# A hybrid decoder layer on one core: the probabilities' transposes split over the two row halves of the array

## The chip, the core and the metric

One program on one core of a Trainium2 chip. TensorE multiplies (a stationary operand is loaded by LDWEIGHTS, a moving one is streamed through) and writes only to PSUM, here eight banks of 128 partitions x 512 float32. VectorE (DVE), ScalarE (ACT) and GpSimd (POOL) do the elementwise work, SyncE (SP) issues the transfers. The metric is the device time of one execution in microseconds, as the median of the runs shown. A profile is the record of one more execution.

## The reference, cut to what matters

One layer of a decoder: a combined input projection, two mixers (gated DeltaNet, and dilated sliding-window attention in three patterns), one output projection, a gated MLP with a short convolution, a final norm. Sequence 1024, width 1024, everything in float32. The change touches the second mixer only: 8 heads of 64, whose three branches are merged by their softmax denominators.

```python
DIL_PATTERNS = ((128, 1), (512, 4), (2048, 16))
BAND_BLOCK = 128

def band_attention(q, k, v, n_back):
    ...
    s = jnp.einsum('...nqd,...nkd->...nqk', qb, kk)
    ...
    s = jnp.where(valid, s, -jnp.inf)
    m = jnp.max(s, axis=-1)
    p = jnp.exp(s - m[..., None])
    den = jnp.sum(p, axis=-1)
    num = jnp.einsum('...nqk,...nkd->...nqd', p, vv)

def dilated_attention(q, k, v):
    ...
    out = num_tot / den_tot[..., None]
```

## The kernel before, in words

**Who sets the order.** The kernel is written as Python generators ("streams": input projection `dense`, delta-rule `chain`, `attention`, `out_proj`, MLP and others), which a small planner, `Weave` (lines 46 to 118), runs against a clock of its own. Each product on TensorE moves that clock by a cost given by hand (`wv.product`); each call on another engine is booked with a cost and a lag until its result is seen (`wv.account`). A stream that yields a number is looked at again when the clock has moved by that much; of all streams that are due, the one with the lowest level goes first. Attention has level 5, `out_proj` 8, `dense` 9. The order in which products are written is TensorE's order on the chip; it is fixed before anything runs. The other engines' order is made by the framework's scheduler from the data dependences, a priority (the wrappers `uv` and `ua` put attention's instructions ahead) and a few orderings written by hand (`after`).

Bookkeeping is by whole tiles: `need(tile)` is the time until the last booked write of a tile can be seen, and a further write to the same tile is booked behind it. VectorE's cost is 0.07 + 0.00105 us per element of a partition, ScalarE's 0.12 + 0.00085, the lag of both 0.28; a product's result is booked as seen 0.25 after it.

**Dense work.** `dense` goes through 25 column tiles of the input projection. Each has two halves of eight steps, and a step is three products of 128 x 128 by 128 x 512 (float32 split into a high and a low part, `mm3`: high x high, high x low, low x high). After each step the stream yields 0.0, so three products are the smallest piece that other streams can come between. They show in the profile as `ps<-xhi,whi`, `ps<-xlo,whi`, `ps<-xhi,wlo`. Four columns of the gate z come last; when a z column is through, `gate` multiplies it into a head's output (`zz`, `og`).

**Attention.** Four head pairs (`pi`), each with eight blocks of 128 queries (`n`), in two groups of four (`hh`), in pairs of blocks (`u` = 0 and 2). A block sees `wd` = 128 to 512 keys: one or two local blocks (`n1`) and `nb` = 0, 1 or 2 blocks of more distant keys, by `CBLOCKS`. The four pairs of blocks of a head pair are thus 128 and 256, 384 and 384, 384 and 384, 512 and 512 keys wide. `advance` pipelines them:

- `turn` (line 969) transposes the probabilities of the pair before, `sm` [queries, keys], to [keys, queries]. For each block (tags `asc` and `atr`) and each of its two heads (`e`) it takes a bank, transposes `wd`/128 squares into it (`tp`, one instruction each, `ps<-ident,sm`: the square is the stationary operand, the identity is streamed), and `turned` copies the local part with VectorE to `pt` and the distant part with ScalarE to `pb`. Ahead of every bank it yields until the block's softmax is due, less 1.0 for the first block and 0.6 for the second (`TSLACK`), so dense steps may come in between.
- `att_values`, once per head pair, transposes the next head pair's values.
- `scores` (line 909) takes four banks, two of each tag, waits until all are free, and multiplies queries by keys, the two heads of the pair on the two row halves of the array (64 rows each), into two banks. Then comes the `softmax` of each block: four fused mask-and-minimum passes on VectorE, four exponentials on ScalarE, four scalings on VectorE.
- `values` (line 983) multiplies the turned probabilities with the values, the two heads on two column halves; after the last pair of a group `merge_classes` adds the distant parts from `pb` (`ps<-pb,vc`), and `give` writes the group out (`oT`).

Each of the tags `asc`, `atr`, `hf`, `ch` has two banks. The four banks of a turn and the four of the next scores are the same four.

**After it.** `mixer_splits` starts when `dense` has written all its products. It splits each head's output into a high and a low part (`ohi`, `olo`), one head after another; inputs 0 to 3 come from the gated heads, 4 to 7 from attention. `out_proj` may start when the last group of attention has begun (`"last group"`): first with the first of its output tiles (j = 0), and with the second (j = 1) only when attention is done. A block of it is one input by one output tile, two halves of three products. In `turned`, for the very last block, three kinds of hand-written orderings hold VectorE's later work behind the last copy: the low parts of the first output weights (`wlo`), the multiplication of the last gate (`og`), and the low parts of all but the first split head (`olo`).

Of the kernel before, what the change touches and what calls it, by code (L numbers as in the profile page):

```python
# [144 lines left out]
def hybrid_layer(tc, I, out):  # L145
# [46 lines left out]
    def tp(dst, src):  # L192
        tc.stamp_issue_order_token(nc.tensor.transpose(dst, src, ident).ins, TOKEN)  # L193
        wv.product(0.11, dst, src)

# [49 lines left out]
    def bank(tag, name="ps"):  # L245
        return tile_(pp_, (P, 512), F32, name, tag, 2)
# [643 lines left out]
    def attention():  # L890
# [64 lines left out]
        def turned(it, e, pt, pp):  # L955
            wd, n1_ = it["wd"], it["n1"]
            inst = uv.tensor_copy(pt[:, :n1_], pp[:, :n1_])
            if it["g"]["pi"] == 3 and it["n"] == 7 and e == 1:

                lows = last.get("wlo", [])  # L960
                last["probabilities"] = inst
                for lo in lows:
                    after(lo, inst, "the probabilities go first")
                for slow in last["og"] + last.get("olo", [])[1:]:
                    after(slow, (lows or [inst])[0], "the first weights go first")
            if it["nb"]:
                ua.activation(it["pb"][e][:, it["u"], :it["nb"]].rearrange("p b t -> p (b t)"), pp[:, n1_:wd], AF.Copy)

        def turn(pair):
            pts = A("pt", "dv*", shape=(P, 4, 256))  # L970
            for b, (it, tag) in enumerate(zip(pair, ("asc", "atr"))):
                sm, wd, n1_ = it["sm"], it["wd"], it["n1"]
                it["pt"] = []
                for e in range(2):
                    pt = pts[:, 2 * b + e, :]
                    it["pt"].append(pt)
                    pp = bank(tag)
                    yield wv.need(pp, sm, slack=TSLACK[b])
                    for i in range(wd // P):
                        tp(pp[:, i * P:(i + 1) * P], sm[:, e, i * P:(i + 1) * P])  # L980
                    turned(it, e, pt, pp)
# [10 lines left out]
        def merge_classes(g):  # L992
# [3 lines left out]
            for c in range(4):  # L996
                for b in range(nb):

                    us = slice(2 if b == nb - 1 else 0, 4)
                    for e in range(2):  # L1000
                        er = slice(64 * e, 64 * e + 64)
                        mm(po[er].rearrange("p (u t) -> p u t", u=4)[:, us, 32 * c:32 * c + 32],
                           vcv[:, c, b, er], g["pb"][e][:, us, b, 32 * c:32 * c + 32], 0.14 if us.start == 0 else 0.08,
# [32 lines left out]
        for pi in range(4):  # L1036
            q, k, vn, vc = cur
            for hh in range(2):
# [5 lines left out]
                pb = [A("pb", "qa", shape=(P, 4, nb, P)) for _ in range(2)]  # L1044
# [50 lines left out]
    def out_proj():  # L1095
# [7 lines left out]
        while todo:  # L1103
# [7 lines left out]
            m, w = MORDER[j], ws[j]  # L1111
            if k == H and not third:
# [610 lines left out]
```

## Time and profile before

| | us |
|---|---|
| median of 3 runs | 1219.16 |
| lowest, highest | 1219.05, 1222.35 |
| the profiled execution | 1219.62 |
| its span | 1217.6 |
| granted TensorE clock over the span | 0.997 |
| attention's head pairs 1 to 4, from the first scores of one to those of the next | 41.9, 41.4, 41.4, 43.1 |
| TensorE busy with transposes in these stretches (line 193, values' transposes included) | 7.36, 7.41, 7.41, 6.37 |

How the rows are read. On the page, "PE" is TensorE's matmuls, "PEld" its weight loads; a busy time is followed by its share of the span and the number of instructions. A timeline row is: start, length, engine, line, operation, output <- inputs by the program's names, shape of the array used (rows*columns) and of the moving operand, and how many instructions the row merges; in brackets stands idle time ahead of it and what ended it. A matmul's length contains its way through the array, so matmuls overlap, and their pace is read from starts. A row of a group is: line, engine, operation, names and shape, count, then busy time, mean length in ns, and idle time before. A row of a stretch is: from:to, length, then for each engine the busy time and (count), the clock, the share of the DMA engines, GB/s. A tile's row is: count, shortest/median/longest ns, first and last start. The chain of waits has start, length, engine and work. Products all stand on line 189 or 193, elementwise work on 139 and 141, because helpers record them.

### The profile page before, as it was taken

The page shows a single profiled execution, that of the slowest core. Times are in us where ns is not written, and L with a number is a line of the kernel's source. Part 1 is how long each engine was busy: PE and PEld are TensorE (multiplying, and loading weights), DVE is VectorE, ACT ScalarE, POOL GpSimd, SP SyncE. Part 2 cuts the span into 40 slices and gives each one's busy share as a digit, 9 for nine tenths or more (in the row PEclk, how much of TensorE's full clock was granted, in tenths as well). Part 3 has the DMA queues.
Part 4 walks back from the last instruction along what each step waited for, and adds up shares of the span by engine and source line. Part 5 has one row for each costly group of instructions (what it writes and reads, how often), then busy time and mean ns, then how long its engine had stood idle before and what let it go on. Part 6 is the DMA issues. An engine that isn't in the chain of part 4 may idle for free.

```text
span 1217.6 us, 17960 instructions
## 1 busy us (share of the span) xinstructions
PE 1202.1 (99%) x6878; PEld 995.2 (82%) x6878; DVE 962.3 (79%) x1531; ACT 576.2 (47%) x1112; POOL 48.0 (4%) x34
## 2 busy tenths in 40 slices
PE   9999999999999999999999999999999999999996
PEld 7888887898777787888788888888888888888886
DVE  7686984474666678667888989888898889898987
ACT  7383344363444344555544445444454454445451
POOL 0212110022000000000000000000000000000000
PEclk9999999999999999999999999999999999999998
DMA  7323235336432312434123131231322296357734
GB/s 234 105 74 101 86 111 167 106 104 216 157 120 90 112 55 97 173 129 151 53 91 99 58 104 60 97 97 59 104 60 97 89 372 222 114 181 224 236 99 142
DMA packets 81846, 153.51 MB, mean 126 GB/s; under 512 B 21568, under 2 KB 32480, under 8 KB 81760
## 3 DMA queue, kind: packets, MB, share of 16 engines
q1 hardware_dynamic: 81760, 152.37, 38.2%
q8 instruction: 54, 0.88, 0.3%
q14 instruction: 32, 0.26, 0.1%
HBM read 114.31 MB, written 35.93 MB: 123 GB/s over the span
## 4 chain that ended last, share of the span: by engine, by line
PE 90%; DVE 4%; DMA 2%; issue 1%; ACT 1%; POOL 0%; SPq 0%; POOLq 0%; DVEq 0%; ACTq 0%
PE ps L189 44%; PE pa L189 19%; PE dw L189 14%; PE pc L189 10%; PE ps L193 3%; DVE x1h L139 1%; DVE pr L139 1%; DMA wst<-in_w 1%; DMA wst<-in_wu 1%; DVE rstdB L139 0%; DVE sm L141 0%; DMA xt<-in_xT 0%; DMA wst<-in_wo 0%; POOL rs L139 0%; DMA wba<-in_wba 0%
## 5 line engine op out<-in xcount | busy, mean ns | idle before, releaser
L189 PE MATMUL dw<-pr 128*128 128x512 f32 (+1 forms) x984 | 211.4, 376 | 0.0
L189 PEld LDWEIGHTS dw<-pr 128*128 128x128 f32 x984 | 176.7, 188 | 33.6
L189 PE MATMUL ps<-xhi,whi 128*128 128x512 f32 x448 | 186.8, 417 | 0.0
L189 PE MATMUL ps<-xhi,wlo 128*128 128x512 f32 x448 | 175.8, 392 | 0.4 <-DVE wlo L139 0.4
L189 PE MATMUL ps<-xlo,whi 128*128 128x512 f32 x448 | 174.8, 390 | 0.0
L189 PE MATMUL pa<-T,pair 128*128 128x512 f32 x528 | 127.1, 389 | 0.0
L189 PEld LDWEIGHTS pa<-T,pair 128*128 128x128 f32 x528 | 99.0, 188 | 20.4
L189 PEld LDWEIGHTS ps<-xhi,wlo 128*128 128x128 f32 x448 | 84.1, 188 | 19.3 <-DVE wlo L139 0.8
L189 PEld LDWEIGHTS ps<-xhi,whi 128*128 128x128 f32 x448 | 84.3, 188 | 16.7 <-issue 2.7
L189 PEld LDWEIGHTS ps<-xlo,whi 128*128 128x128 f32 x448 | 84.6, 189 | 13.2
L139 ACT ACTIVATE u<-pa 128x512 f32<-128x512 f32 x44 | 26.3, 599 | 109.8 <-PE pa L189 109.8
L139 DVE SCALAR_TENSOR_TENSOR y<-xu,fcw,y 128x1023 f32<-128x1023 f32 (+1 forms) x44 | 56.4, 1281 | 25.7 <-ACT y L139 25.6
L139 ACT ACTIVATE pr<-wd 128x1024 fp32r<-128x1024 f32 x33 | 35.0, 1061 | 77.0 <-DVE wd L139 37.5
L139 ACT ACTIVATE whi<-wst 128x1024 fp32r<-128x1024 f32 (+2 forms) x38 | 38.5, 1013 | 67.1 <-PE ps L189 58.9
L189 PE MATMUL pc<-T,S 128*128 128x512 f32 x264 | 63.4, 389 | 0.0
L189 PE MATMUL pa<-T,S 128*128 128x512 f32 x264 | 63.4, 389 | 0.0
L189 PE MATMUL pc<-B,pair 128*128 128x512 f32 x264 | 63.4, 389 | 0.0
L189 PE MATMUL pa<-B,A 128*128 128x512 f32 x264 | 63.4, 389 | 0.0
L139 DVE TENSOR_TENSOR wst<-wst 128x512 f32<-128x512 f32 x88 | 60.4, 686 | 0.8
L189 PE MATMUL ps<-B,pair 128*128 128x512 f32 x252 | 60.5, 389 | 0.0
L141 ACT ACTIVATE sm<-sm,mx 128x384 f32<-128x384 f32 (+3 forms) x64 | 37.8, 592 | 45.5 <-DVE mx L141 45.5
L189 PEld LDWEIGHTS pa<-T,S 128*128 128x128 f32 x264 | 49.6, 188 | 10.3
(235 smaller groups left out, 2275.8 us busy)
## 6 DMA issues: line engine op xcount, KB each, us to landing
wst<-in_wu SPq DMA_DIRECT2D x44, 512.0 KB, 3.7
wd<-in_wd SPq DMA_DIRECT2D x44, 512.0 KB, 4.4
wst<-in_wi SPq DMA_DIRECT2D x25, 512.0 KB, 3.7
upark<-y SPq DMA_DIRECT2D x22, 512.0 KB, 3.7
r<-upark SPq DMA_DIRECT2D x22, 512.0 KB, 9.4
apark<-aqkv SPq DMA_DIRECT2D x12, 512.0 KB, 2.8
wa<-in_wd SPq DMA_DIRECT2D x22, 256.0 KB, 2.9
wst<-in_wo SPq DMA_DIRECT2D x8, 512.0 KB, 3.8
```

Source lines behind the costliest of these rows:

```text
L139: return getattr(eng, op)(*a, **kw)
L141: return getattr(eng, op)(*a, **kw)
L189: tc.stamp_issue_order_token(nc.tensor.matmul(dst, lhs, rhs, start=start, stop=stop, **kw).ins, TOKEN)
L193: tc.stamp_issue_order_token(nc.tensor.transpose(dst, src, ident).ins, TOKEN)
```

## The change

A transpose of 128 queries becomes two of 64, one for the upper and one for the lower 64 rows of `sm` (`HALVES`), each with its own square of the identity (64 x 64). The halves of one block go to its two banks, a bank now holding 64 queries of both heads instead of 128 queries of one. Transposes of the two halves are written alternately, first all of block one, then all of block two, without a yield in between. Ahead of them all stands one wait: until both blocks' softmax is due and the four banks are free, less 0.6. The planner's cost of a half is 0.035. A VectorE copy takes both heads' 64 queries of the local keys; a ScalarE copy takes both heads' 64 queries of one distant key block, so a block with two of them has four such copies instead of two. The tiles `pb` are made per distant block, [keys, 4 blocks, 2 heads, queries], instead of per head. The three orderings behind the last copy are left out when a product of the output projection has already been written.

```diff
--- before.py
+++ after.py
@@ -192,6 +192,11 @@
     def tp(dst, src):
         tc.stamp_issue_order_token(nc.tensor.transpose(dst, src, ident).ins, TOKEN)
         wv.product(0.11, dst, src)
+
+    def tp_half(dst, src, rows):
+
+        tc.stamp_issue_order_token(nc.tensor.transpose(dst, src[rows], ident[rows, rows]).ins, TOKEN)
+        wv.product(0.035, dst, src)
 
     def mm3(dst, lhs, rhs, first, last, **kw):
         us = 0.2135 * rhs[0].shape[-1] / 512
@@ -952,33 +957,43 @@
                 div = uv.tensor_scalar(sm[:, e, :wd], sm[:, e, :wd], den[:, e:e + 1], None, op0=OP.mult)
             return exp, div
 
-        def turned(it, e, pt, pp):
-            wd, n1_ = it["wd"], it["n1"]
-            inst = uv.tensor_copy(pt[:, :n1_], pp[:, :n1_])
-            if it["g"]["pi"] == 3 and it["n"] == 7 and e == 1:
+        def turned(it, h, pts, b, pp):
+
+            nl = it["n1"] // P
+            th = slice(64 * h, 64 * h + 64)
+            inst = uv.tensor_copy(pts[:, 2 * b:2 * b + 2, :it["n1"]].rearrange("p e (i t) -> p e i t", t=P)[:, :, :, th],
+                                  pp[:, :, :nl, :])
+            if it["g"]["pi"] == 3 and it["n"] == 7 and h == 1:
 
                 lows = last.get("wlo", [])
                 last["probabilities"] = inst
-                for lo in lows:
+                for lo in [] if "products" in last else lows:
                     after(lo, inst, "the probabilities go first")
-                for slow in last["og"] + last.get("olo", [])[1:]:
+                for slow in [] if "products" in last else last["og"] + last.get("olo", [])[1:]:
                     after(slow, (lows or [inst])[0], "the first weights go first")
-            if it["nb"]:
-                ua.activation(it["pb"][e][:, it["u"], :it["nb"]].rearrange("p b t -> p (b t)"), pp[:, n1_:wd], AF.Copy)
+            for i in range(it["nb"]):
+                ua.activation(it["pb"][i][:, it["u"], :, th], pp[:, :, nl + i, :], AF.Copy)
 
         def turn(pair):
+            def wait():
+
+                return max(wv.need(pair[0]["sm"], pair[1]["sm"]), *[wv.slot_free(t, n) for t in ("asc", "atr")
+                                                                    for n in (1, 2)]) + TSLACK[1]
+            while wait() > 1e-3:
+                yield wait()
             pts = A("pt", "dv*", shape=(P, 4, 256))
+            banks = []
             for b, (it, tag) in enumerate(zip(pair, ("asc", "atr"))):
-                sm, wd, n1_ = it["sm"], it["wd"], it["n1"]
-                it["pt"] = []
+                it["pt"] = [pts[:, 2 * b + e, :] for e in range(2)]
+                nt = it["wd"] // P
+                banks.append([bank(tag)[:, :2 * nt * 64].rearrange("p (e i t) -> p e i t", e=2, t=64) for _ in range(2)])
+            for b, it in enumerate(pair):
                 for e in range(2):
-                    pt = pts[:, 2 * b + e, :]
-                    it["pt"].append(pt)
-                    pp = bank(tag)
-                    yield wv.need(pp, sm, slack=TSLACK[b])
-                    for i in range(wd // P):
-                        tp(pp[:, i * P:(i + 1) * P], sm[:, e, i * P:(i + 1) * P])
-                    turned(it, e, pt, pp)
+                    for i in range(it["wd"] // P):
+                        for pp, rows in zip(banks[b], HALVES):
+                            tp_half(pp[:, e, i, :], it["sm"][:, e, i * P:(i + 1) * P], rows)
+                for h in range(2):
+                    turned(it, h, pts, b, banks[b][h])
 
         def values(pair):
             yield wv.need(pair[0]["po"], *pair[0]["pt"], slack=-PSLACK)
@@ -1000,7 +1015,7 @@
                     for e in range(2):
                         er = slice(64 * e, 64 * e + 64)
                         mm(po[er].rearrange("p (u t) -> p u t", u=4)[:, us, 32 * c:32 * c + 32],
-                           vcv[:, c, b, er], g["pb"][e][:, us, b, 32 * c:32 * c + 32], 0.14 if us.start == 0 else 0.08,
+                           vcv[:, c, b, er], g["pb"][b][:, us, e, 32 * c:32 * c + 32], 0.14 if us.start == 0 else 0.08,
                            False, c == 3 and b == nb - 1, skip_group_check=True)
 
         def give(g):
@@ -1041,7 +1056,7 @@
                     yield from wv.until(("a", pi + 1, 2))
                     qkv = att_load(pi + 1)
                 po = bank("ch")
-                pb = [A("pb", "qa", shape=(P, 4, nb, P)) for _ in range(2)]
+                pb = [A("pb", "qa", shape=(P, 4, 2, P)) for _ in range(nb)]
                 if pi == 3 and hh == 1:
                     wv.done.add("last group")
                 g = dict(po=po, pb=pb, nb=nb, hh=hh, pi=pi, vc=vc)
@@ -1109,6 +1124,7 @@
             k, j = now[0]
             todo.remove(now[0])
             m, w = MORDER[j], ws[j]
+            last["products"] = True
             if k == H and not third:
 
                 third.extend(A(nm, "qa", F32R) for nm in ("whi", "wlo"))
```

## The prediction, made before the changed kernel was run

> **What bounds the kernel now.** I read the page first, then the table by stretches of time (a stretch is one head pair of the attention), then the timeline of single turns.
>
> ```profile
> PE 1202.1 (99%) x6878; PEld 995.2 (82%) x6878; DVE 962.3 (79%) x1531; ACT 576.2 (47%) x1112; POOL 48.0 (4%) x34
> PE 90%; DVE 4%; DMA 2%; issue 1%; ACT 1%; POOL 0%; SPq 0%; POOLq 0%; DVEq 0%; ACTq 0%
> 351.60:393.00 41.40, 41.40 (x390) 32.83 (x389) 28.32 (x80) 16.66 (x48) 0.00 (x0) 1.00 0.38 122
> 434.40:477.50 43.10, 42.04 (x422) 33.10 (x421) 34.45 (x87) 20.15 (x51) 0.00 (x0) 1.00 0.17 58
> L193 PE MATMUL ps<-ident,sm x184: 270/272/328, 313.4 to 472.0; 128*128 128x128 f32 x184
> ```
>
> TensorE is the bound of the whole and, by this record, of the attention (309.7 to 477.5 us), at full clock. But its work there is of two kinds: the attention's own chain (scores, softmax, turn, copies, next scores), and dense input-projection products that are put wherever the chain waits. I call those the cover. The chain sets when attention ends; the cover sets how much is left behind it. So the change must be priced twice, as TensorE work and as length of the chain.
>
> How much cover remains when the last head pair starts (434.4), and what follows attention:
>
> ```profile
> L189 PE MATMUL ps<-xhi,whi 128*128 128x512 f32 x36 | 15.3, 424 | 0.0
> L189 PE MATMUL ps<-xhi,whi 128*128 128x512 f32 x6 | 2.5, 410 | 0.0
> 481.71 0.39 PE L189 MATMUL ps<-ohi,whi 128*128 128x512 f32 x1
> 482.66 81.99 PE ps L189 x359
> ```
>
> The first row counts 434.4 to 481.75: 36 of each of three kinds, 108 products. The second counts from 477.4: 18 of these run after attention. From 481.71 the output projection's products of the same shape follow; the chain of waits has 359 of them in 81.99 us, 0.228 each. So 18 are 4.1 us.
>
> **The change as TensorE work.** A full transpose, then the two things that a half transpose consists of:
>
> ```profile
> 323.00 0.82 PE L193 MATMUL ps<-ident,sm 128*128 128x128 f32 x6
> 354.81 0.20 PEld L193 LDWEIGHTS ps<-ident,sm 128*128 128x128 f32 x2
> L193 PEld LDWEIGHTS ps<-ident,sm x184: 138/140/143, 313.2 to 471.9; 128*128 128x128 f32 x184
> 309.72 0.52 PEld L189 LDWEIGHTS ps<-kT,qT 64*128 64x128 f32 x8 [0.35 <-issue]
> 329.07 0.64 PE L189 MATMUL ps<-pb,vc 128*64 128x64 f32 x16
> 329.63 0.50 PE L189 MATMUL ps<-xhi,whi 128*128 128x512 f32 x1
> 329.97 0.40 PE L189 MATMUL ps<-xlo,whi 128*128 128x512 f32 x1
> 309.40 0.39 PE L189 MATMUL ps<-xhi,wlo 128*128 128x512 f32 x1
> 309.72 0.93 PE L189 MATMUL ps<-kT,qT 64*128 64x128 f32 x8
> ```
>
> Now: (0.82 - 0.27) / 5 = 0.11 us a transpose, 184 x 0.11 = 20.2 us. Is it the load or the stream that takes 0.11? At 354.81 the array had just been emptied, and the second transposing load follows the first after 0.20 - 0.14 = 0.06 us: the load is not the limit, the stream of 128 identity columns is. Halving it helps, then. The eight score loads at 309.72 are plain loads of the two row halves: four rounds in 0.52, (0.52 - 0.19) / 3 = 0.11 a round, both halves side by side. So row halves do work at the same time. The nearest row for a 64-column stream beside its twin is the merge's: 16 instructions in pairs, (0.64 - 0.22) / 7 = 0.06 a pair. I take 0.06 for a pair of halves: 184 x 0.06 = 11.0, a gain of 9.2 us. Bounds: 0.05 from half of the present stream, 0.12 if the halves run one behind the other.
>
> A turn now leaves the full-array shape and comes back. Entering: from 309.40 the scores start after 0.32 instead of 0.23, 0.09 lost, and the first transposing load stands bare, 0.06. Leaving: the merge's last pair starts at 329.07 + 0.64 - 0.22 = 329.49 and is through at 329.55; the dense product starts at 329.63, and its successor 0.34 later instead of 0.23: 0.08 + 0.11. Together 0.35 us, and there are 16 turns (four lumps per head pair, dense work on both sides): 5.6 us. TensorE saves 9.2 - 5.6 = 3.6 us, 0.9 per head pair; bounds -5.4 and +7.4.
>
> [...]
>
> **The change as length of the chain.** A turn of two 384-wide blocks now, and the softmax ahead of one:
>
> ```profile
> 324.35 0.82 PE L193 MATMUL ps<-ident,sm 128*128 128x128 f32 x6
> 324.80 1.42 DVE L141 COPY pt<-ps 128x256 f32<-128x256 f32 x4
> 326.48 0.49 PE L189 MATMUL ps<-kT,qT 64*128 64x256 f32 x2
> ...
> 358.40 1.73 PE L189 MATMUL ps<-kT,qT 64*128 64x256 f32 x40
> 362.87 1.12 DVE L139 TENSOR_TENSOR aqkv<-ps,rstdB 128x512 f32<-128x512 f32 x1
> 364.05 0.75 DVE L141 TENSOR_SCALAR sm<-sm,mx 128x384 f32<-128x384 f32 x2
> ```
>
> Now block one turns at 323.00, three dense products follow, block two turns at 324.35, six products, next scores at 326.48. After the change nothing turns before block two is due, so the first half of this is no longer hidden: two blocks of three products (6) instead of block one's transposes and 3. Behind the lump stand all four copies. TensorE's order is fixed by the planner's due times, whatever the hardware does: a copy costs 0.07 + 0.00105 x 256 = 0.34 and 0.28 until seen, and four copies into one tile count one behind another. Before, two of them are due 0.33 + 0.25 + 2 x 0.62 = 1.8 after the second turn's start, which asks for its 0.66 and two blocks: the six products seen. After, 0.39 + 0.25 + 4 x 0.62 = 3.1 after the start, which asks for 0.84 and four blocks: 12. So 9 products become 18. The same sum gives +6 for the turn of the narrow first two blocks, +9 for each other one (the one before the next head pair's values included): +33 per head pair, 33 x 0.228 = 7.5 us, less the 0.9 saved: 6.6. Three head pairs grow from 41.4 to 48 each, 19.8 us in all, and use up 99 of the 108 products: the last head pair starts with 9.
>
> The last head pair then runs at the pace of its own latencies.
>
> ```profile
> 434.42 0.93 PE L189 MATMUL ps<-kT,qT 64*128 64x128 f32 x8
> 435.27 1.09 PE L189 MATMUL ps<-pt,vn 128*64 128x128 f32 x16
> 436.19 1.51 PE L189 MATMUL ps<-pb,vc 128*64 128x128 f32 x32
> 437.63 0.44 PE L193 MATMUL ps<-ident,sm 128*128 128x128 f32 x2
> 441.22 0.49 PE L189 MATMUL ps<-kT,qT 64*128 64x256 f32 x2
> ...
> 461.62 2.16 PE L189 MATMUL ps<-kT,qT 64*128 64x256 f32 x40
> 466.16 0.08 DVE L141 DVE_READ_ACCUMULATOR2_ANT mx<- 128x1 f32 x1
> 468.67 0.71 ACT L141 ACTIVATE sm<-sm,mx 128x512 f32<-128x512 f32 x1
> 471.22 1.03 PE L193 MATMUL ps<-ident,sm 128*128 128x128 f32 x8
> ```
>
> For a 384-wide pair: block two's softmax ended 6.4 us after the scores began (358.40 to 364.80), 5.3 without the foreign 1.12; turn 0.85; copies 1.7; 0.15 to re-enter: 8.0. Narrow pair 6.3 (6.8 before, 434.42 to 441.22, with 12 products in it), two at 8.0, and the last to its end 12.5: softmax 7.5 (461.62 to 471.22 is 9.6, of which block two's exponentials lost 2.1 to other work between 466.2 and 468.67), turn 1.3, eight probability copies on ScalarE 2.2, merge 1.5 (436.19 to 437.63); values run under the copies. That is 34.8. Output-projection products are allowed from the last group on; a block of six, 1.37 us, cannot be broken, so I add 2: **37 us** where 43.1 were. Bounds 33.5 and 42: VectorE was busy for 34.45 in this stretch, and the splits of the projection's inputs now fall in it too.
>
> ```profile
> L139 DVE TENSOR_TENSOR olo<-og,ohi x4: 1223/1224/1226, 475.4 to 487.5; 128x1024 fp32r<-128x1024 f32 x4
> L139 DVE TENSOR_TENSOR olo<-ot,ohi x7: 684/692/693, 489.4 to 497.1; 128x512 fp32r<-128x512 f32 x7
> L141 ACT ACTIVATE pb<-ps x48: 277/278/385, 325.3 to 475.6; 128x128 f32<-128x128 f32 x32, 128x256 f32<-128x256 f32 x16
> 472.89 0.91 PE L189 MATMUL ps<-pt,vn 128*64 128x128 f32 x8
> 474.07 0.87 PE L189 MATMUL ps<-pt,vn 128*64 128x128 f32 x7 [0.28 <-DVE pt L141]
> 476.00 1.55 PE L189 MATMUL ps<-pb,vc 128*64 128x128 f32 x30 [0.79 <-ACT pb L141]
> 477.48 0.50 PE L189 MATMUL ps<-xhi,whi 128*128 128x512 f32 x1
> ```
>
> Two full and six half splits more are 2 x 1.22 + 6 x 0.69 = 6.6, so 41 if VectorE does nothing else at the time. Of the refill, seven blocks (inputs 0 to 6, first output tile) can run before attention ends: 7 x 1.37 = 9.6 us; bounds 5.5 (four blocks) and 9.6.
>
> Sum: attention ends 19.8 + (37 - 43.1) = 13.7 later; behind it 4.1 (dense) and 9.6 (refill) are already done: 13.7 - 4.1 - 9.6 = **0.0 us**.
>
> Smaller edits: VectorE's copies keep number and size (64; strides of 64 elements instead of a plain run, hidden under the cover until that is gone, then 0.1 each at most). ScalarE's 16 wide copies become 32 narrow ones, 32 x 0.28 - 16 x 0.38 = 2.9 us, hidden while ScalarE is 40% busy; the last group's are in the 12.5. The probability tiles per block instead of per head, and the wait for four free banks, cost nothing: the banks were read by the softmax some 2 us before. Skipping the three holds when projection products came first (before, the first came at 481.71, after every turn; with the cover gone they come earlier) may let splits of 1.22 ahead of the last copies: 0 to 3.7, inside the bounds of the 37.
>
> The profiled execution took 1219.62; the median shown is 0.46 lower. 1219.6 on its scale is **1219.2** on the median's.
>
> **Rivals.** *Forecast*: cover gone at the last head pair, refill makes it good; chance 0.40, own range 1215.5 to 1222.8 (0.3%, 3.7 us, is about what a measurement here can tell from no change).
>
> *TensorE stays the bound.* If the order gains only one block of three per turn, a head pair grows by 12 x 0.228 - 0.9 = 1.8 us, 7.2 in all, less than the 13.7 of dense work and refill: no new idle time. Then the 3.6 arrive, and about half of the present wait at the end goes too: the values began at 472.89 and the merge's end let dense work on at 477.48, 4.6 us for 2.5 of work (0.92 and 1.44 by the differences at 435.27 to 437.63, 0.1 for a change of shape). 3.6 + 1.1 = 4.7 less, **1214.5**. For it: TensorE shows no idle before 472. Against: the due times above. 0.27.
>
> *Slower: the last head pair is bound by VectorE.* Splits and gates meet the softmax there, the stretch takes 42 and six blocks (8.2) refill: 19.8 - 1.1 - 4.1 - 8.2 = +6.4, **1225.5**; with a refill of 9.6 it decides from 40.6 us on. For it: 80% VectorE in that stretch already (34.45 of 43.1). Against: half of that are gates and weight splits that move ahead with the cover. 0.25.
>
> *No gain per transpose.* If a half's load needed the plain load's 0.11, or the halves ran in turn (0.12), a head pair of 46 would save nothing and pay four times 0.40: growth 7.5 + 1.6 = 9.1, three times 27.3, last stretch 38.6: 27.3 - 4.5 - 4.1 - 9.6 = +9.1, **1228.3**. Against: the 0.06 at 354.81. 0.08. [...]
>
> Faster by over 0.3% 0.27, within 0.40, slower 0.25 + 0.08 = 0.33. The range 1213 to 1228.5 holds the first three with most of their spread.
>
> **What will show it.** Right: 368 half transposes, pairs 0.06 apart, two loads side by side; about 12 dense products between a turn and the next scores; head pairs of some 48 us; hardly a dense product after the third; projection products ahead of the last turn. Wrong: pairs 0.11 apart; head pairs still near 41; dense work after the last turn; or idle TensorE of more than some 8 us in the last head pair.

## The result, and the profile after

| | before | after |
|---|---|---|
| median, us (4 runs each, taken together) | 1220.07 | 1232.21 |
| lowest, highest | 1219.05, 1222.35 | 1231.27, 1233.71 |
| span of the profiled execution | 1217.6 | 1231.6 |
| head pairs 1 to 4, first scores to first scores (the last to the end of attention) | 41.9, 41.4, 41.4, 43.1 | 51.2, 50.8, 47.3, 46.4 |

The change makes the kernel slower: ratio 1.0107, 95% interval 1.0094 to 1.0119. The forecast of no change was wrong, and the time lies above its range too.

From the page of the changed kernel: the busy times, and TensorE's 40 slices.

```profile
PE 1205.2 (98%) x7062; PEld 994.3 (81%) x7062; DVE 961.6 (78%) x1531; ACT 576.5 (47%) x1128; POOL 47.5 (4%) x34
PE   9999999999999988999999999999999999999996
```

The totals hardly differ from before, and yet 14 us are gone. The slices say where: a slice is 1231.6 / 40 = 30.8 us, the 15th and 16th read 8, and they cover 431 to 493 us, the end of the third head pair and most of the last. TensorE is no longer without a break there.

The changed kernel by stretches, one for each head pair (length, then busy time of TensorE, its loads, VectorE, ScalarE, GpSimd with counts, granted clock, share of the DMA engines, GB/s):

```profile
310.10:361.30 51.20, 51.20 (x447) 39.47 (x446) 30.94 (x83) 17.66 (x54) 0.00 (x0) 1.00 0.41 132
361.30:412.00 50.70, 50.70 (x481) 39.47 (x480) 32.90 (x86) 18.61 (x54) 0.00 (x0) 1.00 0.35 117
412.00:459.30 47.30, 45.14 (x454) 34.90 (x453) 35.09 (x88) 22.20 (x54) 0.00 (x0) 1.00 0.19 60
459.30:505.70 46.40, 36.61 (x418) 28.17 (x418) 32.06 (x88) 20.67 (x63) 0.00 (x0) 0.82 0.28 91
```

In the first two TensorE is busy throughout, and still they take 9 us more than before: they hold more products. In the third it runs short, and in the last it is idle for 46.4 - 36.6 = 9.8 us. VectorE, at 32 of 46, is not full either; so the last stretch is a chain of waits, not one engine's work. And its granted clock is 0.82, of which the last section tells.

What the first stretches hold more of is seen in the groups of the second head pair, first of the kernel before (351.6 to 393.0), then of the changed one (361.3 to 412.0):

```profile
L189 PE MATMUL ps<-xhi,whi 128*128 128x512 f32 x33 | 14.1, 426 | 0.0
```

```profile
L189 PE MATMUL ps<-xhi,whi 128*128 128x512 f32 x48 | 19.7, 411 | 0.0
```

33 dense steps of three products became 48: 45 products more. The first head pair has 45 more too (156 for 111), the third only 18 more (117 for 99), because the dense products end in it. The turn itself, on TensorE's timeline of the changed kernel, with what stands before and behind it:

```profile
378.06 0.39 PE L189 MATMUL ps<-xhi,wlo 128*128 128x512 f32 x1
378.38 0.96 PE L198 MATMUL ps<-ident,sm 64*128 64x64 f32 x24
379.27 0.50 PE L189 MATMUL ps<-xhi,whi 128*128 128x512 f32 x1
379.61 0.40 PE L189 MATMUL ps<-xlo,whi 128*128 128x512 f32 x1
...
382.21 0.92 PE L189 MATMUL ps<-kT,qT 64*128 64x256 f32 x6
```

24 halves take 0.89 us, and 12 dense products follow until the next scores at 382.21. VectorE and ScalarE were done well before that:

```profile
376.27 0.75 DVE L141 TENSOR_SCALAR sm<-sm,mx 128x384 f32<-128x384 f32 x2
379.40 1.40 DVE L141 COPY pt<-ps 128x256 f32<-128x256 f32 x4
379.85 1.26 ACT L141 ACTIVATE pb<-ps 128x128 f32<-128x128 f32 x4 [4.60 <-DVE pt L141]
```

The second block's probabilities were ready at 377.02, the turn began at 378.38; VectorE's last copy ended at 380.80 and ScalarE's at 381.11, the scores began at 382.21. That is 1.4 us of slack ahead of one turn and 1.1 behind its copies, filled with dense products. The hardware was not late; the order was.

### The profile page after: what moved, and what is told of

Same layout as the page of the kernel before. It is cut to its first block, busy times and chain, and to the rows that moved or that the text cites. A ratio compares the mean times of both kernels' runs of the same rounds, so it can differ in the third digit from the quotient of the medians.

```text
span 1231.6 us, 18320 instructions
## 1 busy us (share of the span) xinstructions
PE 1205.2 (98%) x7062; PEld 994.3 (81%) x7062; DVE 961.6 (78%) x1531; ACT 576.5 (47%) x1128; POOL 47.5 (4%) x34
## 4 chain that ended last, share of the span: by engine, by line
PE 89%; DVE 5%; DMA 2%; ACT 1%; issue 1%; POOL 0%; SPq 0%; POOLq 0%; DVEq 0%; ACTq 0%
PE ps L189 44%; PE pa L189 19%; PE dw L189 14%; PE pc L189 9%; PE ps L193 2%; DVE x1h L139 1%; DVE pr L139 1%; PE ps L198 1%; DVE sm L141 1%; DMA ot<-mixer 1%; DMA xt<-in_xT 1%; DMA wst<-in_wu 1%; DVE rstdB L139 0%; ACT sq L139 0%; ACT xhi L139 0%
## 5 line engine op out<-in xcount | busy, mean ns | idle before, releaser
L189 PEld LDWEIGHTS ps<-xhi,wlo 128*128 128x128 f32 x448 | 84.1, 188 | 19.1 <-DVE wlo L139 0.9
L189 PEld LDWEIGHTS ps<-xlo,whi 128*128 128x128 f32 x448 | 84.5, 189 | 13.8
L139 ACT ACTIVATE whi<-wst 128x1024 fp32r<-128x1024 f32 (+2 forms) x38 | 38.5, 1013 | 70.5 <-PE ps L189 56.0
L141 ACT ACTIVATE sm<-sm,mx 128x384 f32<-128x384 f32 (+3 forms) x64 | 37.8, 592 | 51.1 <-DVE mx L141 51.0
```

The lines of the kernel that those rows point to most:

```text
L139: return getattr(eng, op)(*a, **kw)
L141: return getattr(eng, op)(*a, **kw)
L189: tc.stamp_issue_order_token(nc.tensor.matmul(dst, lhs, rhs, start=start, stop=stop, **kw).ins, TOKEN)
```

## The experiments

A time is the median, a ratio is against the kernel before, run beside it on the same chip. That kernel's own median lay between 1218.73 and 1220.07 in these groups of runs, so versions of different groups are best compared by their distance from it. Three causes were held against one another at first: **L**, the lump (both blocks turned in one go) lengthens the chain and uses up the cover; **P**, the halves themselves cost, through their changes of shape; **S**, in the last head pair VectorE stands at the splits of the projection's inputs while the copies of a turn wait behind them.

### 1. Halves, but each block turned by itself (e1_apart)

```diff
-                return max(wv.need(pair[0]["sm"], pair[1]["sm"]), *[wv.slot_free(t, n) for t in ("asc", "atr")
-                                                                    for n in (1, 2)]) + TSLACK[1]
...
             for b, (it, tag) in enumerate(zip(pair, ("asc", "atr"))):
+                def wait():
+                    return max([wv.need(it["sm"])] + [wv.slot_free(tag, n) for n in (1, 2)]) + TSLACK[b]
+                while wait() > 1e-3:
+                    yield wait()
```

> Half transposes kept, but the two blocks of a pair turn apart again: each block waits for its own softmax (less 1.0 and 0.6) and its own two banks, and dense steps may come between. Theory L (the lump lengthens attention's chain, the cover runs out): head pairs go from 51 back to 42 to 45 us, dense products remain at the start of the last head pair, total 1219 to 1225. Rival P (the halves with their changes of shape are what costs): 32 changes instead of 16, so no better than the changed kernel, 1232 to 1238. Rival S (the last head pair's stall behind the splits on VectorE is what costs): first three head pairs stay near 51, total 1225 to 1232.

Measured: 1233.1 us (1232.05 to 1233.9), ratio 1.0115 (1.0098 to 1.0132). L's number missed by far, and the time alone lies in P's range of 1232 to 1238; the next run decides about P. The head pairs shrank to 46.5, 46.6 and 47.3, so part of the growth was indeed the lump's, but not to 41: 9 products stand behind a second turn where there were 6, and 6 between the two turns where there were 3. The last one took 49.4 us, with one wait of TensorE above all:

```profile
PE ps L198 <- DVE sm L141: 5.3, 2, 5.1
```

(a row of waits: engine and tile, what it waited for, us in total, times, the longest). So the lump is not the only thing that lengthens the chain, and a head pair without cover is expensive in this version as well.

### 2. The lump, but with whole transposes (e2_lump_whole)

The edit as seen from the changed kernel; banks, copies and `pb` are per head again, as in the kernel before.

```diff
-                        for pp, rows in zip(banks[b], HALVES):
-                            tp_half(pp[:, e, i, :], it["sm"][:, e, i * P:(i + 1) * P], rows)
+                        tp(banks[b][e][:, i * P:(i + 1) * P], it["sm"][:, e, i * P:(i + 1) * P])
```

> The lump alone: both blocks of a pair in one go after one wait, but with the whole 128 x 128 transposes, banks and copies per head of the kernel before. L: head pairs of 50 to 53 us as in the changed kernel, cover gone before the fourth, total 1229 to 1238. P: near the kernel before, 1218 to 1223. S: as L if the splits meet the copies again, so it is not told apart here.

Measured: 1231.21 us (1230.1 to 1233.13), ratio 1.0104 (1.0089 to 1.0119). The halves are gone and the loss has stayed. P falls: nothing that row halves cost on TensorE explains the 12 us.

### 3. Copies booked side by side (e3_due_copies)

The planner books a write to a tile behind the tile's booked write before it, lag included. Here the four copies into `pt` are booked by VectorE's own time alone, which moves the next scores' due time forward.

```diff
+            name = pts.tensor.name
+            seen = wv.ready.get(name, 0.0)
+            if (b, h) != (0, 0):
+                wv.ready[name] = 0.0
             inst = uv.tensor_copy(pts[:, 2 * b:2 * b + 2, :it["n1"]] ...
+            wv.ready[name] = max(wv.ready[name], seen)
```

> The changed kernel, with the planner booking the four copies of a turn one behind another on VectorE without adding 0.28 us until seen between them (they write different parts of one tile). Only the order on TensorE changes: the next scores are due some 0.8 us earlier. L: 9 instead of 12 dense products between a turn and the next scores, head pairs about 3 us shorter (48), more cover left, total 1222 to 1229. P: no change, 1231 to 1234. S: 1229 to 1234, since the splits still run ahead of the copies in the last head pair.

Measured: 1227.52 us (1226.76 to 1232.22), ratio 1.008 (1.0061 to 1.01). 9 products stand behind a turn instead of 12, the first two head pairs are 2.1 and 2.7 us shorter, attention ends at 499.66 instead of 505.75, and in the covered head pairs no copy was late. About a quarter of the loss came from a due time that the hardware did not need.

### 4. Splits written after attention (e6_splits_late)

```diff
             else:
+                yield from wv.until("attention")
                 src = A("ot", "ev")
```

> The changed kernel, but the splits of the output projection's inputs 4 to 7 (which wait for a load) are not written before attention is done; inputs 0 to 3 may still refill. S: the wait of 4.9 us for the copies in the last head pair goes and little refill is lost, total 1223 to 1228. L: the head pairs before stay at 51, what the stall gives back is lost again in refill (24 instead of 42 products, 4.1 us), total 1229 to 1235. P: no change, 1231 to 1234.

Measured: 1236.97 us (1236.11 to 1240.32), ratio 1.0155 (1.014 to 1.017), slower than the changed kernel by 4.8 us as the times stand and by 6.1 by their distances from the kernel before, outside what any of the three causes expected. It did not test S: the framework's scheduler put the splits ahead of the copies on VectorE all the same, and the wait stayed, as the waits of its last head pair show:

```profile
PE ps L189 <- DVE pt L141: 4.2, 1, 4.2
```

What it did change is the refill: only 24 projection products came before the end of attention instead of 42. The 18 that are missing are 18 x 0.228 = 4.1 us by the prediction's refill term, which is most of what the time grew by.

### 5. Splits held behind the first turn's copies by hand (e9_splits_behind_copies)

```diff
+            if it["g"]["pi"] == 3 and it["n"] == 1 and h == 1:
+                last["early"] = inst
+                wv.done.add("early")
...
+                yield from wv.until("early")
...
+                    for inst in (first_hi, late):
+                        after(inst, last["early"], "the probabilities go first")
```

> TensorE's order is that of the changed kernel, instruction for instruction; on VectorE the four splits olo<-ot of the last head pair, and on ScalarE their ohi, stand behind the four copies of that head pair's first turn instead of ahead of them. Theory S (the splits on VectorE, which wait for a transfer, cost the stall of 4.9 us in front of the next scores): that stall goes, though part of it comes back where the splits now stand ahead of the next softmax; attention ends 2 to 5 us earlier, near 502, and the time is 1227 to 1230.5, against 1232.2. Rival (the stall only stands where another would: the out-projection's products or the next softmax wait for the same transfer): the idle time of TensorE in the last head pair stays at 9.8 us and the time within 1231 to 1234.

First the changed kernel at that place, from its timeline (SPq is the transfer queue; the times in brackets are idle time and what ended it):

```profile
463.12 7.93 SPq L139 DMA_DIRECT2D ot<-mixer  x5
467.68 0.59 PE L198 MATMUL ps<-ident,sm 64*128 64x64 f32 x12
468.65 2.63 ACT L139 ACTIVATE ohi<-ot 128x512 fp32r<-128x512 f32 x4 [3.10 <-DMA ot<-mixer]
469.31 2.69 DVE L139 TENSOR_TENSOR olo<-ot,ohi 128x512 fp32r<-128x512 f32 x4 [2.76 <-ACT ohi L139]
471.92 1.05 DVE L139 COPY oT<-ps 128x512 f32<-128x512 f32 x1
472.81 1.13 DVE L141 COPY pt<-ps 128x128 f32<-128x128 f32 x4
473.14 1.41 PE L189 MATMUL ps<-kT,qT 64*128 64x256 f32 x4 [4.87 <-DVE pt L141]
```

The turn is through at 468.27. VectorE has stood since 466.55, 2.76 us in all, for a split: the split needs `ohi` from ScalarE, and ScalarE waited 3.10 us for the transfer of `ot`. Then VectorE does four splits, and only then the copies that free the banks. TensorE stands for 4.87 us. The same place with the splits held back:

```profile
467.00 0.59 PE L198 MATMUL ps<-ident,sm 64*128 64x64 f32 x12
468.03 1.12 DVE L141 COPY pt<-ps 128x128 f32<-128x128 f32 x4
468.36 2.15 PE L189 MATMUL ps<-kT,qT 64*128 64x256 f32 x40 [0.76 <-DVE pt L141]
469.08 2.48 DVE L139 TENSOR_TENSOR olo<-ot,ohi 128x512 fp32r<-128x512 f32 x4
```

The wait fell from 4.87 to 0.76, the last head pair from 46.4 to 41.0 us, and the time to 1228.37 us (1227.51 to 1229.94), ratio 1.0077 (1.0064 to 1.0091): 3.8 us less than the changed kernel as the times stand, 2.9 by their distances from the kernel before, and inside what S expected. TensorE's order is the same in both, so this is S alone. Of the 5.4 us that the last head pair is shorter, 4.1 are the wait itself; part of the rest is the clock of the last section: from the scores behind the wait to the values it is 3.23 us in the changed kernel (granted clock 0.50) and 2.08 here (1.00).

### 6. Due time 1.3 us earlier (e4_due_early)

```diff
-TSLACK = -1.0, -0.6
+TSLACK = -1.0, -1.9
```

> The changed kernel with the turn of both blocks placed 1.3 us earlier in the planner's order (-1.9 for -0.6). By the order, the dense products of a head pair fall from 156 to 111, as many as before the change (9 between a turn and the next scores, 21 to 27 from the scores to the turn), so the 108 products of cover that the change used up should last into the last head pair's third turn. Theory D (the due times in the planner set the chain, not the hardware: a turn's input lay ready 1.4 us before it began): head pairs near 41 to 43 us, attention ends at 478 to 484, idle time of TensorE falls, 1216 to 1223. Rival H (VectorE and ScalarE can't deliver 1.3 us earlier): TensorE waits over 0.5 us for sm at most of the 16 turns, the head pairs stay above 47 us, 1228 or more.

Measured: 1219.1 us (1216.57 to 1228.82), ratio 1.001 (0.9986 to 1.0033): one number in the planner takes the whole loss back. Its second head pair by groups, and two of its stretches:

```profile
L189 PE MATMUL ps<-xhi,whi 128*128 128x512 f32 x37 | 15.4, 417 | 0.0
```

```profile
353.40:396.70 43.30, 43.30 (x448) 33.28 (x447) 30.08 (x82) 17.20 (x50) 0.00 (x0) 1.00 0.38 132
...
441.20:483.70 42.50, 40.51 (x458) 30.22 (x457) 36.14 (x90) 23.18 (x61) 0.00 (x0) 0.96 0.29 89
```

111 dense products where the changed kernel had 144; that the kernel before had as many, as expected, is not so in this head pair: it had 99 (111 in its first, where this version has 123). The head pairs take 43.7, 43.3, 44.5 and 42.5 us, a little above the 41 to 43 of theory D; the end of attention and the time are within it. The cover lasts into the last head pair, whose idle time falls from 9.8 to 2.0 us. And the rival's waits do not appear. This is all that TensorE waited for from the first scores to the end of attention:

```profile
PE ps L189 <- ACT pb L141: 1.5, 2, 1.1
PE ps L198 <- DVE sm L141: 0.4, 1, 0.4
```

With turns 1.3 us earlier, TensorE stood for probabilities once in 16 turns.

### 7. Both due times (e5_due_early_copies), and earlier still (e11_due_earlier)

Run 6 and run 3 together; then the same with -2.2 for -1.9.

> As the run before with the copies booked side by side too, so that 6 dense products stand between most turns and the next scores: 102 per head pair, 9 fewer than before the change, and dense outlasts attention. Theory D: head pairs near 40 to 42 us, attention ends at 472 to 480, no idle time for want of products; what is left of the change is TensorE's own saving of 3.6 us, 1213.5 to 1219. Rival H: the six products (1.4 us) don't cover the copies, TensorE waits over 1 us at each of the 16 turns, 1224 or more.

> As the version at -1.9 with copies side by side, the due time another 0.3 us earlier (-2.2): 3 dense products fewer between the scores and two of the turns of a head pair. If the hardware still has slack there, the time stays at 1214 to 1217, since dense outlasts attention in either and a shorter chain buys nothing more; if the softmax is now late, TensorE waits for sm before these turns, up to 0.3 us at 8 of them, and the time is 1216 to 1219.

Measured: 1215.64 us (1213.95 to 1217.09), ratio 0.9972 (0.996 to 0.9983), and 1215.2 us (1213.84 to 1216.35), ratio 0.9965 (0.9952 to 0.9978). Both are a little faster than the kernel before, and the step from one to the other is worth nothing that can be told. The second head pair of the first of them:

```profile
351.80:393.00 41.20, 41.20 (x439) 31.61 (x438) 28.12 (x80) 16.46 (x52) 0.00 (x0) 1.00 0.40 127
L189 PE MATMUL ps<-xhi,whi 128*128 128x512 f32 x34 | 14.3, 420 | 0.0
```

102 dense products, 41.2 us: the chain of the kernel before. Attention ends at 474.66, with 15 dense products still behind it.

### 8. The same due times with whole transposes (e10_whole_due_early)

> The version with due times at -1.9 and the copies booked side by side, but with whole transposes of 128 queries in place of the halves; the lump of both blocks stays. The order has 99 dense products per head pair, against 102 with halves, so the chain is about as short and cover lasts past attention in both; what differs is the transposing itself: 184 whole ones for 368 halves. Term of the prediction (184 transposes cost 0.05 us more each than a pair of halves, 9.2, less 16 shape changes of 0.35, 5.6): with halves TensorE is 3.6 us shorter, so this one takes 1217.5 to 1221, against 1215.6. Rival (the shape changes eat the saving, and the gain of that version over before is the lump's and the due times' alone): 1214 to 1217, no difference.

Measured: 1217.57 us (1215.99 to 1219.59), ratio 0.998 (0.9971 to 0.9989), 2.4 us above the version with halves that ran beside it (e11_due_earlier, whose due time is 0.3 us earlier still). That is at the very edge between the two expectations. The turn of two 384-wide blocks, here with whole transposes and below with halves (e5_due_early_copies):

```profile
323.58 0.39 PE L189 MATMUL ps<-xhi,wlo 128*128 128x512 f32 x1
323.81 1.47 PE L193 MATMUL ps<-ident,sm 128*128 128x128 f32 x12
325.04 0.47 PE L189 MATMUL ps<-xhi,whi 128*128 128x512 f32 x1
325.35 0.39 PE L189 MATMUL ps<-xlo,whi 128*128 128x512 f32 x1
```

```profile
323.95 0.39 PE L189 MATMUL ps<-xhi,wlo 128*128 128x512 f32 x1
324.27 0.96 PE L198 MATMUL ps<-ident,sm 64*128 64x64 f32 x24
325.16 0.50 PE L189 MATMUL ps<-xhi,whi 128*128 128x512 f32 x1
325.50 0.40 PE L189 MATMUL ps<-xlo,whi 128*128 128x512 f32 x1
```

From the last dense product ahead of the turn to the second one behind it: 325.35 - 323.58 = 1.77 us whole, 325.50 - 323.95 = 1.55 in halves. A turn of 12 transposes gains 0.22 us. The narrow turn of 6 loses 0.06 (1.18 for 1.12) and the turn of 16 gains 0.42 (1.79 for 2.21), so a head pair gains 0.8 and the four 3.2 us. The turns show that the halves save time on TensorE. How much of it arrives in the whole is less sure: 2.4 us against e11_due_earlier, 1.1 against e5_due_early_copies by the distances from the kernel before (2.4 and 3.5).

### 9. The kernel before with the earlier due time (b4_before_due_early)

> The kernel before, without halves and lump, with its second block's due time at -1.9 for -0.6 and nothing else. Theory: the kernel before turns block one by itself and sets block two behind its copies, so its order gains nothing from the earlier due time; cover already outlasts attention by 4.1 us, so 1217 to 1224. Rival: the earlier due time alone is what made the changed kernel fast, and the kernel before gains as much: below 1216.

Measured: 1218.71 us (1216.86 to 1224.29), ratio 0.999 (0.9977 to 1.0004). Its attention ends at 469.16, 8.3 us earlier than before, and 48 dense products follow: it only moved cover from ahead of the end to behind it. The due time alone is no clear gain. The expectation had the order wrong, though: with block two due at -1.9 this kernel turns both blocks in one piece too (rows of 12 whole transposes, with no dense product between them), and its first, second and fourth head pairs take 38.5, 37.8 and 38.3 us instead of 41.9, 41.4 and 43.1 (the third, 46.2 us, holds a run of 48 dense products). So turning both blocks at once does not lengthen the chain by itself; the due time that goes with it does.

### One sum for all of them

The prediction's way of counting can be put to all the runs: the end of attention (where the product behind the last merge starts), plus 0.228 for each dense product left behind it, less 0.228 for each projection product ahead of it, against 477.48 + 4.1 = 481.6 of the kernel before.

| run | attention ends | dense behind | projection ahead | sum against before | median against before |
|---|---|---|---|---|---|
| after | 505.75 | 0 | 42 | +14.6 | +12.1 |
| e1_apart | 501.27 | 0 | 18 | +15.6 | +14.4 |
| e2_lump_whole | 502.02 | 0 | 42 | +10.8 | +12.5 |
| e3_due_copies | 499.66 | 0 | 36 | +9.9 | +8.8 |
| e6_splits_late | 506.21 | 0 | 24 | +19.1 | +18.2 |
| e9_splits_behind_copies | 500.54 | 0 | 42 | +9.4 | +9.3 |
| e4_due_early | 483.76 | 0 | 12 | -0.6 | 0.0 |
| e5_due_early_copies | 474.66 | 15 | 0 | -3.5 | -3.5 |
| e11_due_earlier | 472.59 | 24 | 0 | -3.5 | -4.8 |
| e10_whole_due_early | 474.89 | 21 | 0 | -1.9 | -2.4 |
| b4_before_due_early | 469.16 | 48 | 0 | -1.5 | -1.3 |

All eleven agree within 2.5 us; the ends and counts are those of one profiled execution each. So the losses of 9 to 18 us lie in this one place of the kernel. For the gains of 1 to 5 us the sum is too coarse to show as much.

## Why the prediction was wrong, by its own steps

**TensorE's work: right.** A pair of halves at 0.06 us and a change of shape at 0.35 made a gain of 12 x 0.05 - 0.35 = 0.25 us for a turn of 12 transposes; 0.22 was measured. What was put down to the changes of shape is seen in the rows at 378.06 to 379.61: the turn starts 0.32 after the dense product ahead of it instead of 0.23, and the second dense product behind it follows the first by 0.34. Only a little of the latter is the change of shape, since a turn of whole transposes has 0.31 there (run 8). The rest of its price lies in the turn itself: between turns of 12 and of 32 halves its length grows by 0.061 us a pair (0.53 to 1.14 in the changed kernel, at 315.97 and 357.19), so 12 pairs would be 0.73, and 0.89 were measured. That these 0.16 us belong to the change of shape is the author's reading; no run varied it alone. Over the whole kernel 3.6 us were forecast; the turns add up to 3.2, the times of run 8 give 1.1 to 2.4.

**Products behind a turn: right.** 12 were forecast between a turn and the next scores, and 12 are there.

**Products ahead of a turn: the first step that failed.** The prediction wrote "two blocks of three products (6) instead of block one's transposes and 3", 3 more per turn, from durations on the chip. The planner does not know these. In the kernel before, block one was written up to 1.0 us ahead of its booked due time, and block two 0.6 ahead of its own; `wv.product` then moves the planner's clock to the due time, and in that stretch of its clock no dense product is placed. With the lump this happens once, with 0.6. The time given up comes back as products, so the turns begin later: ahead of the four turns of the second head pair stand 9, 27, 21 and 30 products (before, up to block two's transposes, 6, 18, 15 and 24), 24 more, where the forecast's 3 for each turn make 12. So +33 products per head pair became +45, and the first two head pairs grew by 9.3 and 9.4 us instead of 6.6. The third, where the cover ran out, grew by 5.9; together that is 24.6 us, not 19.8. That reading of the code is argued; what run 6 shows is that the due time holds the products there, and that the hardware has room for 1.3 us less.

**"The cover is used up": right, but earlier.** 9 products were to be left for the last head pair; the last dense ones run at 454.6 us, ahead of the third pair's last turn.

**"Last head pair 37 us": the larger failure.** It took 46.4. By its own four parts (scores to next scores) the forecast was 6.3, 8.0, 8.0 and 12.5, and 2 for projection blocks. Measured, from the scores at 459.34, 473.14, 485.81 and 492.91 to the end at 505.75: 13.8, 12.7, 7.1 and 12.8. The last two came near; the last had luck in it, as 1.6 us of it are the slower clock of the last section, which the forecast did not have. Of the 7.5 us that the first is too long, run 5 takes back 4.9, and 4.1 of these are the wait behind the splits. Another wait of the same kind is still there in run 5: ahead of the second half of the scores, at 462.12, TensorE stood 1.97 us, because VectorE split weights and multiplied a gate (from 458.90 on) and came to the last two copies of the turn before only at 461.17. The slower clock adds 1.6 us to it (values and merge, last section). For the second, two rows more:

```profile
480.54 0.75 DVE L141 TENSOR_SCALAR sm<-sm,mx 128x384 f32<-128x384 f32 x2
483.34 0.96 PE L198 MATMUL ps<-ident,sm 64*128 64x64 f32 x24
```

The softmax ended at 481.29, which is 8.1 us after its scores and not 5.3 to 6.4: the scores themselves were slow (3.23 us at a granted clock of 0.50), and a split and its copy on ScalarE came between. Then the turn waited 2.05 us for TensorE, which was in a run of 24 projection products (477.67 to 483.34) that the order had put there as one piece. The turn (0.89) and six more products (1.58) make up the 12.7. Run 5 takes the first part's wait away and comes to 41.0, inside the bounds of 33.5 to 42, but by other parts than forecast (8.9, 11.1, 7.1 and 14.0). The prediction did name the splits ("may let splits of 1.22 ahead of the last copies"), but as a cost of VectorE's time at the last turn; what cost was that a split waits for a transfer and stands in front of the first turn's copies in VectorE's order. And it priced every product of this stretch at the pace of covered ones. The three orderings that the change leaves out at the last turn were not put back in any run; the part in which they act took 12.8 for 12.5.

**Refill: right.** 42 products, 9.6 us.

**The sum.** 24.6 + 3.3 + 0.4 (a later start) - 4.1 - 9.6 = +14.6 instead of 0.0: 4.8 from the first three head pairs, through the products ahead of the turns, 9.4 from the last head pair, 0.4 from the start.

**The rivals.** The slower one, a last head pair held up by VectorE, had the right place and the right actors, with 42 us for it and not 46.4; its price was too low because it counted busy time and no waits. "TensorE stays the bound" at 1214.5 is not what this kernel does, but it is what the versions with earlier due times do: 1215.6 and 1215.2. "No gain per transpose" is refuted by the turns of run 8, 1.55 us for 1.77.

## What to carry to other kernels

Where an order is written down ahead of time, a change that merges two waits changes due times, and those must be worked out in the planner's own arithmetic, not from durations on the chip; then look whether the engines sit finished before each step, since that slack may be taken back in one number, as here. Ahead of pricing a latency-bound stretch, list what stands in front of the critical instruction in its engine's queue, and whether any of that waits for a transfer, as a split's input did here for 3.10 us. Filler work had two prices here: its time on the engine, 0.228 us a product, and what happened in the stretch that no longer had any, 46.4 us for 43.1.

## What the runs showed of the hardware

**Behind five stretches in which TensorE was partly idle its granted clock was 0.50, and the same work took longer.** The changed kernel's last head pair, in pieces of 3.41 us: the clock is seen to change at 460.36, 467.19, 470.60, 477.43, 494.49 and 497.90, which lie 3.41 us or a multiple of it apart (after the length, TensorE's busy time, and before the last two columns the granted clock):

```profile
456.95:460.36 3.41, 2.02 (x33) 1.56 (x29) 3.41 (x8) 2.66 (x8) 0.00 (x0) 1.00 0.22 48
460.36:463.77 3.41, 1.65 (x6) 1.00 (x8) 3.41 (x10) 1.93 (x9) 0.00 (x0) 0.50 0.38 67
463.77:467.19 3.42, 3.42 (x39) 3.42 (x41) 2.75 (x10) 1.78 (x5) 0.00 (x0) 0.50 0.92 326
467.19:470.60 3.41, 1.08 (x26) 0.88 (x22) 1.28 (x2) 1.85 (x3) 0.00 (x0) 1.00 0.77 264
470.60:474.01 3.41, 0.87 (x4) 0.87 (x6) 3.34 (x8) 1.19 (x3) 0.00 (x0) 0.50 0.30 99
474.01:477.43 3.42, 3.42 (x49) 2.38 (x48) 2.02 (x6) 0.78 (x3) 0.00 (x0) 0.50 0.40 136
...
491.08:494.49 3.41, 2.33 (x24) 1.71 (x20) 2.40 (x8) 1.11 (x4) 0.00 (x0) 1.00 0.23 80
494.49:497.90 3.41, 3.41 (x47) 2.15 (x48) 0.90 (x2) 0.63 (x1) 0.00 (x0) 0.50 0.23 74
497.90:501.32 3.42, 2.35 (x24) 1.59 (x22) 3.20 (x11) 2.92 (x8) 0.00 (x0) 1.00 0.00 0
501.32:504.73 3.41, 2.65 (x51) 2.17 (x52) 2.37 (x7) 1.48 (x9) 0.00 (x0) 1.00 0.02 5
```

Read each row's clock against the busy time of the row ahead of it. In this stretch, after 2.02, 1.65, 1.08, 0.87 and 2.33 us of work in 3.41 the clock is 0.50 for the next 3.41; after a full one it is back at 1.00 (467.19, 477.43, 497.90). That TensorE is busy without a break at 0.50 (463.77, 474.01, 494.49) shows that this is a pace and not a way to write idle time. What it costs is seen where the same 52 instructions run at 1.00 and at 0.50, from the scores to the first product behind the values:

```profile
369.52 1.73 PE L189 MATMUL ps<-kT,qT 64*128 64x256 f32 x40
371.99 0.50 PE L189 MATMUL ps<-xhi,whi 128*128 128x512 f32 x1
...
473.14 3.30 PE L189 MATMUL ps<-kT,qT 64*128 64x256 f32 x40 [4.87 <-DVE pt L141]
477.67 0.50 PE L189 MATMUL ps<-ohi,whi 128*128 128x512 f32 x1
```

2.47 us against 4.53. In the last head pair this comes three times; the other two are 1.6 us each (values and merge from 463.61 to 467.68, 4.07 us, where the same instructions take 1.02 + 1.44 at 1.00, the first at 453.62, the second in the kernel before at 436.19; the second kind of scores and the values from 494.53 to 498.15, 3.62 against 2.05 at 452.59 to 454.64). An estimate from these three is 5 us in all. Of the versions with earlier due times, e4_due_early has 0.96 over its last head pair and e5_due_early_copies 1.00; e10_whole_due_early and e11_due_earlier have 1.00 over the whole attention. It was not varied by itself: no run kept TensorE busy with other work in that place, so the order of events is shown and the cause is not. Nor can a busy time be named as the bound: in this trace 2.33 us of work in 3.41 at 491.08 were followed by 0.50, and 2.35 at 497.90 and 2.07 at 600.30 (30 pieces further on, if they run on to there) by 1.00. What decides it stays open.
